# Token-major feed-forwards, output projections and gates in a two-block network on one core

## The chip, the core and the metric

The kernel runs on one core of one Trainium2 chip. The metric is device microseconds of one execution. The engines are TensorE (PE; PEld is its weight-load side), VectorE (DVE), ScalarE (ACT), GpSimd (POOL) and SyncE (SP), whose queue starts all loads here.

## What is computed

256 tokens of 1024 features pass through a block of one layer and a block of two, all in float32. Each `swiglu` is a feed-forward with 2816 inner features; the first block normalises before and after each part, the second only before.

```python
def swiglu(x, w_gate, w_up, w_down):
    return (jax.nn.silu(x @ w_gate) * (x @ w_up)) @ w_down
# first block
f = swiglu(rms_norm(h, ffn1_pre_norm[l]), ffn1_w_gate[l], ffn1_w_up[l], ffn1_w_down[l])
h = h + FFN_RESIDUAL_WEIGHT * rms_norm(f, ffn1_post_norm[l])
mixed = hybrid_mixer(rms_norm(h, mix_pre_norm[l]), ...)       # 8-head attention, 4-head delta rule
h = h + rms_norm(mixed @ w_out[l], mix_post_norm[l])
c = memory_cross_attention(rms_norm(h, mem_pre_norm[l]), rms_norm(mem, mem_kv_norm[l]), ...)  # ends with @ w_o
h = h + rms_norm(c, mem_post_norm[l])
f = swiglu(rms_norm(h, ffn2_pre_norm[l]), ...)
h = h + FFN_RESIDUAL_WEIGHT * rms_norm(f, ffn2_post_norm[l])
# second block, each of two layers
h = h + 0.5 * swiglu_2(rmsnorm(h, ffn1_norm[i]), ffn1_wg[i], ffn1_wu[i], ffn1_wd[i])
h = h + hybrid_mixer_2(rmsnorm(h, mix_norm[i]), ...)
h = h + 0.5 * swiglu_2(rmsnorm(h, ffn2_norm[i]), ffn2_wg[i], ffn2_wu[i], ffn2_wd[i])
gate = jax.nn.sigmoid(rmsnorm(h, ple_norm[i]) @ ple_w_gate[i])
h = h + gate * (p[i] @ ple_w_proj[i])
return rmsnorm(h, final_norm)
# inside hybrid_mixer_2: short convolution and a chunked state-space scan (ssd), then
merged = jax.nn.sigmoid(gate_a) * y_a + jax.nn.sigmoid(gate_m) * y_m   # y_a = .. @ sc_w_out, y_m = .. @ m_w_out
return merged @ w_o
```

## The kernel before

**Layout.** Activations lie feature-major: the residual `h` is eight tiles [128 features, 256 tokens]. A product of the large kind takes each operand in two float32r parts, `hi` and `lo` (`split` for activations, `wunit` for weights), and adds three passes: hi·hi, hi·lo, lo·hi (`mm3`, L325). The weights are stationary, 128 by 128, and 256 tokens stream past them; the sum lands in a PSUM tile [128, 256] of the pool `pm` (four banks). A few products (`proj_tok`, L369: the values of the two attentions) already have tokens on partitions.

**Weights.** `wunit` (L283) loads 512 KB, [128, 4 row chunks, 256 columns], copies it to `hi` on ACT (L297) and subtracts on DVE (L298). There are four raw buffers and three of `hi` and `lo`. The Tile framework orders all instructions by priority, which is program order; units are taken `AHEAD` = 60 places early. `preload` (L306) takes the first units of the next stage further ahead, into tiles of the arena `R`.

**Stages.** `ffn` (L470) goes over 11 column blocks, two 256-column blocks of gate and up at a time; for each 128 features DVE multiplies by the spread reciprocal root `rb`, ACT takes silu, DVE multiplies, ACT and DVE split. The down product then runs over 22 row chunks. `residual` (L508) adds a product to `h`. `post` (L514) is the first block's norm after a part: `evict` squares each chunk, `finish` scales it, adds it to `h` and splits `h` for the next stage.

**Root mean squares.** Features lie on partitions, so squares are summed with one-column products on PE (`rstd` L399, `sum_squares` L439); POOL raises to the power -1/2, and `spread` (L416) multiplies with the identity to bring the 256 token values to every partition.

**Fillers.** Work that waits for nothing stands in the program where a norm is pending: `mem_k` after the first feed-forward and after `w_out`, `ple_proj(0)` after `mem_w_o`, `ple_proj(1)` after the first block's last feed-forward.

**Arenas.** Fixed tiles are handed out in program order: `S` [128, 256], `D` pairs of them, `R` pairs in float32r. `scope` adds tiles for a part.

Of the kernel before, what the change touches and what calls it, by code (L numbers as in the profile page):

```python
# [23 lines left out]
# columns of the packed per-feature vectors (one column per 128 features)  # L24
# [10 lines left out]
# rows that every partition holds  # L35
# [54 lines left out]
# how many places of the program order a weight unit is taken ahead, how many one that preload() takes,  # L90
# and how many places products that wait for other engines are put back
AHEAD = 60
PRELOAD = 120
# [3 lines left out]
class Arena:  # L97
    """fixed tiles, handed out and taken back in program order"""
# [22 lines left out]
    def get(self, keep=False):  # L121
        """keep: a tile that outlives the parts added last"""
# [14 lines left out]
class Net:  # L137
    def __init__(self, ctx, tc, a):
# [12 lines left out]
        self.S.add(ap, 36)  # L151
# [9 lines left out]
        self.ones = {n: self.cst.tile([P, 1], F32, name=f"ones{n}") for n in (1, 128, 512, 1024)}  # L161
        nc.gpsimd.memset(self.ones[1], 1.0)
        for n in (128, 512, 1024):
            self.act(self.ones[n], self.ones[1], AF.Copy, scale=1.0 / n)
        self.h = self.start()
        self.ident = self.c("ident")
        nc.sync.dma_start(self.ident, a["con"][:, :P])
# [5 lines left out]
    def constants(self):  # L173
# [7 lines left out]
        # masks and selectors, exact in bfloat16  # L181
# [11 lines left out]
    def start(self):  # L193
        """the activations in the order that the first products need them, with the first weights between"""
        nc, a = self.nc, self.a
        h = [self.S.get() for _ in range(KC)]
        first = [(a[f"ffn1_w_{q}"], ks) for ks in self.steps(KC) for q in ("gate", "up")]
        self.ahead, units = [], []
        for i in range(3):
            src, ks = first[i]  # L200
# [3 lines left out]
            units.append(self.wunit(src[0, :, ks[0]:ks[-1] + 1, :], len(ks), False, 2 if i == 0 else 1))  # L204
            for c in range(max(4 * i, 1), min(4 * i + 4, KC)):
                nc.sync.dma_start(h[c], a["xT"][c * P:(c + 1) * P, :])
        self.ahead = units[::-1]
        return h

# [15 lines left out]
    def t(self, tag, shape, dtype=F32, bufs=2, part=False):  # L225
        """scratch: the next of bufs fixed tiles; part: only there within the current scope"""
# [8 lines left out]
    def half(self):  # L235
        """scratch [P, 256]: halves of the two t tiles in turn"""
# [11 lines left out]
    def late(self, *names):  # L248
        """products that wait for other engines, put behind others that are ready"""
# [33 lines left out]
    def wunit(self, src, a, prio=True, cut=1):  # L283
        """hi/lo parts of src [P, a, 256], in cut pieces"""
# [3 lines left out]
        n = a * S  # L288
# [3 lines left out]
        with self.tc.high_priority(AHEAD) if prio else nullcontext():  # L292
            for c in range(cut):
                j, e = c * a // cut, (c + 1) * a // cut
                r, o, d = (q[:, j * S:e * S] for q in (raw, hi, lo))
# [3 lines left out]
        parts = [x[:, :n].rearrange("p (a b) -> p a b", a=a) for x in (hi, lo)]  # L299
        return [[q[:, j] for q in parts] for j in range(a)], []  # L300

    def first(self, *src):
        """the units that come first when the first blocks of src are taken in step"""
        return [(q, 0, ks) for ks in self.steps(KC) for q in src]

    def preload(self, *units):  # L306
        """the parts of units (src, block, row chunks), which are the next to be used, in tiles of the arena"""
        nc, out = self.nc, []
        for src, b, ks in units:
            n = len(ks)  # L310
            with self.tc.high_priority(PRELOAD):
                raw = self.wp.tile([P, 1024], F32, tag="raw", name="raw", bufs=4)
                nc.sync.dma_start(raw[:, :n * S].rearrange("p (a b) -> p a b", a=n), src[b, :, ks[0]:ks[-1] + 1, :])
                tiles = [self.split(raw[:, j * S:(j + 1) * S], keep=True) for j in range(n)]
            out.insert(0, ([[t[:, 0, :], t[:, 1, :]] for t in tiles], tiles))
        return out

    def units(self, src, b, K):
        """the weight units of column block b of src [blocks, P, K, 256]: row chunks, hi/lo parts"""
        for ks in self.steps(K):  # L320
            w, tiles = self.wunit(src[b, :, ks[0]:ks[-1] + 1, :], len(ks))
            yield ks, w
            self.R.put(*tiles)
# [8 lines left out]
    @staticmethod  # L332
    def steps(K):
        """the row chunks of each weight unit"""
        return [range(k, min(k + 4, K)) for k in range(0, K, 4)]
# [10 lines left out]
    def proj(self, src, b0, nblk, x, evict, wide=False, last=False):  # L346
        """evict(chunk, ps) with ps [P, 256]: out features on partitions; wide: the first two blocks in step;
        last: the chunks of the last block one after the other"""
        u = 0
        while u < nblk:  # L350
            if last and u == nblk - 1:
                units = list(self.units(src, b0 + u, len(x)))
                for f in range(2):
                    ps = self.mbank()[:, :S]
                    for ks, w in units:
                        for k, wk in zip(ks, w):
                            self.mm3(ps, wk, x[k], k == 0, k == len(x) - 1, f * P)
                    evict(2 * u + f, ps)
                return
# [8 lines left out]

    def proj_tok(self, src, b0, nblk, x, evict):  # L369
        """evict(blk, t, ps) with ps [P, 256]: tokens of tile t on partitions"""  # L370
        K = len(x)
        for u in range(nblk):
            banks = [self.mbank()[:, :S] for _ in range(2)]
            for ks, w in self.units(src, b0 + u, K):
                for t in range(2):
                    for k, (wh, wl) in zip(ks, w):
                        xh, xl = x[k][:, 0, t * P:(t + 1) * P], x[k][:, 1, t * P:(t + 1) * P]
                        self.mm(banks[t], xh, wh, k == 0, False)
                        self.mm(banks[t], xl, wh, False, False)
                        self.mm(banks[t], xh, wl, False, k == K - 1)  # L380
# [9 lines left out]
    def sq_acc(self, acc, src):  # L390
        """acc + src*src for src [P, 256] (acc None to begin)"""
# [1083 lines left out]
```

## Time and profile before

| | us |
|---|---|
| median of 3 runs | 2219.32 |
| lowest and highest run | 2210.61, 2225.4 |
| span of the profiled execution, first to last instruction | 2217.7 |
| PE busy in it | 2195.2 |

The page gives the profiled execution by its span only; that is 1.6 us under the median run. Busy PE time counts modelled ends, so a stretch in which PE is busy throughout can still issue its products at different rates: rates are read as time over count.

### The profile page before, as it was taken

To read this page: it belongs to the slowest core of one execution; us is meant where nothing else is said; L and a number is where in the kernel's file an instruction comes from. 1 tells how busy PE (TensorE), PEld (TensorE's weight loads), DVE (VectorE), ACT (ScalarE), POOL (GpSimd) and SP (SyncE) were. 2 spreads that over 40 slices of the span, in tenths; PEclk is the share of its full clock that TensorE was granted. 3 is DMA by queue.
4 is the path that set the end of the run, shared out by engine and by line. 5 is a ranking of instruction groups with operands and counts; after the bars stand their busy time and mean duration, and the time that the engine had idled before them with its cause. 6 is when DMAs were issued, how large, how long until landed. Compare 5 with 4: busy or idle time off the path is not lost.

```text
span 2217.7 us, 45480 instructions
## 1 busy us (share of the span) xinstructions
PE 2195.2 (99%) x18672; PEld 2152.2 (97%) x18672; DVE 1558.5 (70%) x2608; ACT 1185.1 (53%) x2033; POOL 43.3 (2%) x54
## 2 busy tenths in 40 slices
PE   8999999999999999999999999999999999999998
PEld 8999997999999999998999999999999999999998
DVE  6756873667665766798766766676669886767666
ACT  6545633555454544567555554454457755645444
POOL 0000000000000000000000000000000000000000
PEclk9999997999999999999999999999999999999999
DMA  7565520435556556553455556655665436555563
GB/s 255 177 185 169 166 77 1 166 121 162 189 184 191 173 188 186 186 186 106 157 189 185 192 190 195 190 182 195 190 196 187 136 125 193 179 193 193 193 188 127
DMA packets 110369, 379.44 MB, mean 171 GB/s; under 512 B 12368, under 2 KB 17104, under 8 KB 110160
## 3 DMA queue, kind: packets, MB, share of 16 engines
q1 hardware_dynamic: 110160, 376.53, 52.9%
q8 instruction: 146, 2.39, 0.4%
q14 instruction: 63, 0.52, 0.1%
HBM read 375.43 MB, written 1.05 MB: 170 GB/s over the span
## 4 chain that ended last, share of the span: by engine, by line
PE 95%; DVE 2%; ACT 1%; DMA 1%; issue 0%; POOL 0%; SPq 0%; DVEq 0%; ACTq 0%; POOLq 0%
PE pm L265 84%; PE px L265 11%; PE px L268 1%; DVE lo L298 1%; DVE s L259 0%; DMA raw<-in_ffn_w_up_dram 0%; DMA raw<-in_ple_w_gate_dram 0%; ACT hi L297 0%; DMA raw<-in_ffn_wu_dram 0%; DVE r L259 0%; ACT d L262 0%; PE pm L268 0%; ACT L262 0%; DVE acc L256 0%; DVE w L253 0%
## 5 line engine op out<-in xcount | busy, mean ns | idle before, releaser
L265 PE MATMUL pm<-r,hi 128*128 128x256 f32 x10640 | 1861.5, 279 | 7.2 <-ACT hi L297 5.7
L265 PEld LDWEIGHTS pm<-r,hi 128*128 128x128 f32 x10640 | 1621.7, 189 | 9.5 <-ACT hi L297 5.7
L265 PE MATMUL pm<-r,lo 128*128 128x256 f32 x5320 | 1484.4, 279 | 1.6 <-DVE lo L298 1.6
L298 DVE TENSOR_TENSOR lo<-raw,hi 128x1024 fp32r<-128x1024 f32 (+1 forms) x718 | 861.0, 1200 | 488.3 <-ACT hi L297 484.4
L297 ACT CAST hi<-raw 128x1024 fp32r<-128x1024 f32 (+1 forms) x718 | 739.1, 1030 | 731.5 <-PE pm L265 576.5
L265 PEld LDWEIGHTS pm<-r,lo 128*128 128x128 f32 x5320 | 1001.4, 188 | 3.2 <-DVE lo L298 2.2
L276 ACT CAST r<-w 128x256 fp32r<-128x256 f32 x136 | 54.5, 403 | 61.0 <-DVE w L253 61.0
L253 DVE TENSOR_TENSOR t<-pm,rb 128x512 f32<-128x512 f32 (+1 forms) x132 | 80.4, 636 | 0.2
L262 ACT ACTIVATE r<-s,vec 128x256 fp32r<-128x256 f32 x136 | 66.1, 504 | 22.1 <-DVE s L259 18.2
L262 ACT ACTIVATE sq<-s 128x256 f32<-128x256 f32 x152 | 60.3, 410 | 27.6 <-DVE s L253 19.8
L259 DVE SCALAR_TENSOR_TENSOR s<-pm,vec,s 128x255 f32<-128x255 f32 x144 | 68.9, 479 | 2.8
L259 DVE SCALAR_TENSOR_TENSOR r<-s,vec,r 128x256 fp32r<-128x256 f32 x136 | 65.5, 499 | 5.0 <-ACT r L262 4.4
L265 PE MATMUL px<-r,hi 128*128 128x256 f32 x384 | 66.9, 279 | 0.0
L277 DVE TENSOR_TENSOR r<-w,r 128x256 fp32r<-128x256 f32 x136 | 57.0, 422 | 8.1
L265 PEld LDWEIGHTS px<-r,hi 128*128 128x128 f32 x384 | 58.5, 189 | 0.0
L265 PE MATMUL px<-r,lo 128*128 128x256 f32 x192 | 53.5, 278 | 0.0
L413 POOL TENSOR_TENSOR rs<-rv,mhalf 128x2 f32<-128x2 f32 x26 | 23.4, 898 | 1504.2 <-DVE rv L411 1504.2
L262 ACT ACTIVATE w<-t 128x256 f32<-128x256 f32 x132 | 48.1, 409 | 7.1 <-DVE t L253 7.1
L253 DVE TENSOR_TENSOR w<-w,t 128x256 f32<-128x256 f32 x132 | 50.1, 418 | 0.3 <-ACT w L262 0.2
L265 PE MATMUL px<-d,d 128*64 128x128 f32 (+2 forms) x384 | 42.7, 291 | 0.2
L256 DVE TENSOR_TENSOR acc<-acc,sq 128x256 f32<-128x256 f32 x94 | 39.4, 420 | 4.4 <-ACT sq L262 1.9
L262 ACT ACTIVATE d<-px,nac 128x128 f32<-128x128 f32 x128 | 36.4, 375 | 3.2 <-PE px L265 2.9
(231 smaller groups left out, 1371.8 us busy)
## 6 DMA issues: line engine op xcount, KB each, us to landing
raw<-in_w_in_dram SPq DMA_DIRECT2D x188, 512.0 KB, 3.8
raw<-in_ffn_wg_dram SPq DMA_DIRECT2D x88, 512.0 KB, 4.5
raw<-in_ffn_wu_dram SPq DMA_DIRECT2D x88, 512.0 KB, 4.5
raw<-in_ffn_wd_dram SPq DMA_DIRECT2D x80, 512.0 KB, 4.0
raw<-in_ffn_w_up_dram SPq DMA_DIRECT2D x44, 512.0 KB, 4.5
raw<-in_ffn_w_gate_dram SPq DMA_DIRECT2D x43, 512.0 KB, 4.6
raw<-in_ffn_w_down_dram SPq DMA_DIRECT2D x40, 512.0 KB, 3.6
raw<-in_m_w_out_dram SPq DMA_DIRECT2D x32, 512.0 KB, 4.4
```

The lines of the kernel that those rows point to most:

```text
L253: self.nc.vector.tensor_tensor(out=out, in0=a, in1=b, op=ALU.mult)
L256: self.nc.vector.tensor_tensor(out=out, in0=a, in1=b, op=ALU.add)
L259: self.nc.vector.scalar_tensor_tensor(out=out, in0=a, scalar=s, in1=b, op0=op0, op1=op1)
L262: self.nc.scalar.activation(out, a, f, **kw)
L265: self.nc.tensor.matmul(out, lhsT=lhsT, rhs=rhs, start=start, stop=stop)
L268: self.nc.tensor.transpose(out, a, self.ident[:k, :k])
L276: nc.scalar.copy(hi, src)
L277: nc.vector.tensor_tensor(out=lo, in0=src, in1=hi, op=ALU.subtract)
L297: nc.scalar.copy(o, r)
L298: nc.vector.tensor_tensor(out=d, in0=r, in1=o, op=ALU.subtract)
L413: self.nc.gpsimd.tensor_tensor(out=r, in0=v, in1=self.mhalf[:, :2], op=ALU.pow)
```

## The change

Feed-forwards, `w_out`, `mem_w_o`, the two attentions' values, the second mixer's two gates, `sc_w_out`, `m_w_out`, `w_o` and the embedding gate and projection become token-major: `tblock` takes 128 tokens of an activation chunk as the stationary operand and streams 512 weight columns into a whole PSUM bank, once for each half of the tokens. Gate and up columns are laid side by side in memory (`beside`). The residual `h` becomes two tiles [128 tokens, 1024]. Sums of squares become a by-product of an ACT square (`sq_row`), and the reciprocal root is a per-partition scalar (`rstd_row`) that ACT or DVE applies at eviction, without `spread`. Where the next product needs features on partitions, PE transposes (`turn`, `close`). Gains of the norms after a part come as a row broadcast to all partitions (`row`). `preload` goes; `ple_proj(1)` moves from the end of the first block to ahead of the second layer. The projections into the mixers (`proj`), the memory's queries and keys, and the scans stay feature-major. Lines of the diff that only drop comments are left out.

```diff
-        self.S.add(ap, 36)
+        self.S.add(ap, 12)
+        self.T = Arena("tk", [P, D], F32)
+        self.T.add(ap, 6)
...
+            units.append(self.wunit(a["ffn1_gu"][0, :, ks[0]:ks[-1] + 1, :], False, 2 if i == 0 else 1))
+            for c in range(max(2 * i, 1), 2 * i + 2):
                 nc.sync.dma_start(h[c], a["xT"][c * P:(c + 1) * P, :])
+            for c in range(2 * i, 2 * i + 2):
+                x.append(self.split(h[c], self.v("ffn1_pre_norm", c)))
...
+        for t in range(2):
+            nc.sync.dma_start(self.h[t], a["x"][t * P:(t + 1) * P, :])
...
-    def preload(self, *units):
-        """the parts of units (src, block, row chunks), which are the next to be used, in tiles of the arena"""
-        nc, out = self.nc, []
...
+        step = 1024 // src.shape[3]
...
+    def tblock(self, src, b, x, banks):
+        K = len(x)
+        for ks, w in self.units(src, b, K):
+            for t in range(2):
+                s = slice(t * P, (t + 1) * P)
+                for k, (wh, wl) in zip(ks, w):
+                    xh, xl = x[k][:, 0, s], x[k][:, 1, s]
+                    self.mm(banks[t], xh, wh, k == 0, False)
+                    self.mm(banks[t], xl, wh, False, False)
+                    self.mm(banks[t], xh, wl, False, k == K - 1)
+            yield ks
...
+    def turn(self, src, c):
+        ps = self.bank()
+        for j in range(2):
+            for t in range(2):
+                self.transpose(ps[:, j * S + t * P:j * S + (t + 1) * P], src[t][:, (c + j) * P:(c + j + 1) * P])
+        return ps.rearrange("p (j s) -> p j s", j=2)
...
-    def rstd(self, acc, n, mult=1.0):
...
+    def sq_row(self, ss, t, n, src, mult=1.0):
+        junk = self.t("junk", [P, W], bufs=1)
+        self.act(junk, src, AF.Square, scale=(mult / D) ** 0.5, accum_out=ss[:, n, t:t + 1])
+    def rstd_row(self, ss, mult=1.0):
...
+        self.stt(v, ss[:, 0], EPS * mult, ss[:, 1], ALU.add, ALU.add)
         r = self.t("rs", [P, 2])
         self.nc.gpsimd.tensor_tensor(out=r, in0=v, in1=self.mhalf[:, :2], op=ALU.pow)
         return r
...
+    def turned(self, src, gain=None):
+        x = []
+        for c in range(0, KC, 2):
+            ps = self.turn(src, c)
+            x += [self.split(ps[:, j], None if gain is None else self.v(gain, c + j), True) for j in range(2)]
+        return x
...
+    def row(self, name):
+        g = self.t("grow", [P, D], bufs=1)
+        self.nc.sync.dma_start(g, self.a["rows"][self.a["row_of"][name]:self.a["row_of"][name] + 1, :].to_broadcast([P, D]))
...
+    def lend(self, n):
+        tiles = [self.T.get() for _ in range(n)]
+        new = [t[:, j * W:(j + 1) * W].rearrange("p (a s) -> p a s", a=2) for t in tiles for j in range(2)]
+        self.D.free[:0] = new
+        self.D.parts.append(new)
...
-    def ffn(self, x, acc, wg, wu, wd, evict, mid=None):
-        with self.scope(NF, 0, 0):
-            rb = self.rstd_b(acc, D)
-            rbb = rb[:, None, :].to_broadcast([P, 2, S])
...
+    def ffn(self, x, ss, wgu, wd, evict, mid=None):
+        with self.scope(0, 0, 0) as pool:
+            with self.late("rstd"):
+                r = self.rstd_row(ss)
...
+            def close(gt):
+                ps = self.bank()
+                for f in range(2):
+                    for t in range(2):
+                        self.transpose(ps[:, f * S + t * P:f * S + (t + 1) * P], gt[:, t, f * P:(f + 1) * P])
+                n = len(g)
+                d = pool.tile([P, 2, 2, S], F32R, tag=f"g{n}", name=f"g{n}", bufs=1)
+                psv = ps.rearrange("p (f s) -> p f s", f=2)
+                self.nc.scalar.copy(d[:, 0], psv)
+                self.nc.vector.tensor_tensor(out=d[:, 1], in0=psv, in1=d[:, 0], op=ALU.subtract)
+                g.extend([d[:, :, 0], d[:, :, 1]])
+            last = None
...
-                for f in range(2):
...
-                    g.append(self.split(sg))
+                banks = [self.mbank() for _ in range(2)]
+                for ks in self.tblock(wgu, u, x, banks):
+                    if ks[0] == 2 and last is not None:
+                        close(last)
+                gt = self.t("t", [P, 2, S])
+                for t in range(2):
+                    self.act(gt[:, t], banks[t][:, :S], AF.Silu, scale=r[:, t:t + 1])
+                    self.stt(gt[:, t], banks[t][:, S:], r[:, t:t + 1], gt[:, t], ALU.mult, ALU.mult)
+                last = gt
                 if mid and u in mid:
                     mid[u]()
...
+            banks = [self.mbank() for _ in range(2)]
+            g += [None, None]
+            gg = Late(g, lambda: (g.__delitem__(slice(-2, None)), close(last)))
+            for d in range(D // W):
+                if d:
+                    banks = [self.mbank() for _ in range(2)]
+                for _ in self.tblock(wd, d, gg, banks):
+                    gg.settle()
+                for t in range(2):
+                    evict(d, t, banks[t])
...
-        """evict that adds scale*ps to h in place"""
-        def evict(c, ps):
-            self.stt(h[c], ps, scale, h[c], ALU.mult, ALU.add)
+        def evict(n, t, ps):
+            o = h[t][:, n * W:(n + 1) * W]
+            self.stt(o, ps, scale, o, ALU.mult, ALU.add)
...
-            f = self.S.get()
-            self.nc.vector.tensor_scalar(out=f, in0=ps, scalar1=self.v(gain, c), scalar2=None, op0=ALU.mult)
-            st["f"].append(f)
...
+        st = dict(f=[self.T.get() for _ in range(2)], ss=self.t("ss", [P, 2, 2]), g=self.row(gain))
+        def evict(n, t, ps):
+            s = slice(n * W, (n + 1) * W)
+            self.sq_row(st["ss"], t, n, ps, mult)
+            self.mul(st["f"][t][:, s], ps, st["g"][:, s])
...
+            r = self.rstd_row(st["ss"], mult)
+            ss = self.t("ss", [P, 2, 2])
...
+            for n in range(2):
+                s = slice(n * W, (n + 1) * W)
+                for t in range(2):
+                    self.stt(h[t][:, s], st["f"][t][:, s], r[:, t:t + 1], h[t][:, s], ALU.mult, ALU.add)
+                for c in range(4 * n, 4 * n + 4, 2):
+                    ps = self.turn(h, c)
+                    x += [self.split(ps[:, j], self.v(gain, c + j), True) for j in range(2)]
+                for t in range(2):
+                    self.sq_row(ss, t, n, h[t][:, s])
...
+        for t in range(2):
+            nc.vector.tensor_scalar(out=hn[t], in0=h[t], scalar1=r[:, t:t + 1], scalar2=None, op0=ALU.mult)
...
+        def ga_evict(n, t, ps):
+            self.act(ya[t][:, n * W:(n + 1) * W], ps, AF.Tanh, scale=rh[:, t:t + 1])
+        self.proj_tok(a["w_in_2_gates"][i], 0, 1, xu, ga_evict)
+        x = self.turned(hn, "mix_norm_2" + L)
+        self.T.put(*hn)
+        self.proj_tok(a["w_in_2_gates"][i], 1, 1, xu, lambda n, t, ps: ga_evict(1, t, ps))
...
+        def ym_evict(n, t, ps):
+            o = gm[t][:, n * W:(n + 1) * W]
+            self.stt(o, o, 1.0, ps, ALU.add, ALU.mult)
+            self.add(o, o, ya[t][:, n * W:(n + 1) * W])
+            if t:
+                for c in range(4 * n, 4 * n + 4, 2):
+                    p2 = self.turn(gm, c)
+                    merged.extend(self.split(p2[:, j]) for j in range(2))
+        self.proj_tok(a["m_w_out_2"][i], 0, 2, yn, ym_evict)
+        self.T.put(*gm, *ya)
         self.R.put(*yn)
-        self.proj(a["w_o_2"][i], 0, 4, merged, self.residual(h, 0.5))
...
-            mixed = self.mixer1(h, *x)
+            with self.lend(6):
+                mixed = self.mixer1(h, *x)
             ev, fin = self.post("mix_post_norm", 1.0)
...
-        w = self.preload(*self.first(a["ffn1_wg_2"][0], a["ffn1_wu_2"][0])[:2])
-        self.ple_proj(1)
-        self.ahead = w
+        self.ffn(*x, a["ffn2_gu"], a["ffn2_w_down"], ev)
         return fin(h, "ffn1_norm_2.0")
...
+        if i:
+            n.ple_proj(1)
+            x = n.pre(h, f"ffn1_norm_2.{i}")
...
+    for b in range(2):
+        for t in range(2):
+            n.sq_row(ss, t, b, h[t][:, b * W:(b + 1) * W])
+    r = n.rstd_row(ss)
+    for b in range(2):
+        for t in range(2):
+            o = h[t][:, b * W:(b + 1) * W]
+            n.stt(o, o, r[:, t:t + 1], g[:, b * W:(b + 1) * W], ALU.mult, ALU.mult)
+            nc.sync.dma_start(out[t * P:(t + 1) * P, b * W:(b + 1) * W], o)
...
+    def beside(g, u):
+        *lead, k, m = g.shape
+        both = [q.reshape(*lead, k, m // S, 1, S) for q in (g, u)]
+        return np.concatenate(both, axis=-2).reshape(*lead, k, 2 * m)
```

## Rows read from the trace of the kernel before

**Rows 1.** The page, part 1: busy time of each engine.

```profile
PE 2195.2 (99%) x18672; PEld 2152.2 (97%) x18672; DVE 1558.5 (70%) x2608; ACT 1185.1 (53%) x2033; POOL 43.3 (2%) x54
```

**Rows 2.** The page, part 4: shares of the chain that ended last, by engine.

```profile
PE 95%; DVE 2%; ACT 1%; DMA 1%; issue 0%; POOL 0%; SPq 0%; DVEq 0%; ACTq 0%; POOLq 0%
```

**Rows 3.** Windows: stretch, length, each engine's busy us and instructions, PEclk, DMA, GB/s.

```profile
60.00:202.00 142.00, 142.00 (x1205) 141.88 (x1205) 89.67 (x124) 67.53 (x98) 0.26 (x1) 1.00 0.59 183
...
415.00:437.00 22.00, 22.00 (x194) 21.83 (x193) 16.62 (x30) 12.93 (x22) 0.00 (x0) 1.00 0.58 191
...
729.00:925.00 196.00, 196.00 (x1668) 196.00 (x1667) 130.15 (x183) 96.92 (x145) 3.26 (x2) 1.00 0.58 182
...
1190.00:1278.00 88.00, 88.00 (x779) 88.00 (x778) 60.13 (x91) 44.20 (x65) 1.39 (x2) 1.00 0.58 192
...
1484.00:1660.00 176.00, 176.00 (x1555) 176.00 (x1554) 117.27 (x159) 89.80 (x130) 2.59 (x1) 1.00 0.61 193
...
2014.00:2188.00 174.00, 174.00 (x1537) 173.99 (x1536) 115.09 (x156) 86.97 (x126) 0.00 (x0) 1.00 0.61 193
```

**Rows 4.** Groups of PE instructions, shapes apart: busy us, mean ns, idle before.

```profile
L265 PE MATMUL pm<-r,hi 128*128 128x256 f32 x10640 | 1861.5, 279 | 7.2 <-ACT hi L297 5.7 <-DVE r L259 0.9 <-ACT r L262 0.6
...
L265 PE MATMUL px<-ones,acc 128*128 128x1 f32 x152 | 20.5, 228 | 0.8 <-DVE acc L256 0.8
...
L265 PE MATMUL px<-con,rs 128*128 128x128 f32 x100 | 18.1, 284 | 2.5 <-POOL rs L413 2.5
...
L268 PE MATMUL px<-con,s 128*128 128x128 f32 x80 | 11.6, 274 | 0.0
...
L265 PE MATMUL px<-ones,sq 128*128 128x1 f32 x72 | 10.9, 256 | 1.4 <-ACT sq L262 1.4
...
L265 PE MATMUL px<-d,d 128*128 128x256 f32 x32 | 7.4, 379 | 0.0
```

**Rows 5.** Timeline of PE, three stretches: start, us, instruction, count.

```profile
246.04 1.39 PE L265 MATMUL px<-ones,sq 128*128 128x1 f32 x12
...
486.75 3.19 PE L265 MATMUL px<-d,d 128*128 128x256 f32 x14
...
1009.56 0.71 PE L268 MATMUL px<-con,s 128*128 128x128 f32 x5
```

**Rows 6.** What PE waited for: us in total, times, longest.

```profile
PE pm L265 <- ACT hi L297: 5.7, 1, 5.7
```

**Rows 7.** Groups of ACT, DVE and POOL instructions, shapes apart.

```profile
L298 DVE TENSOR_TENSOR lo<-raw,hi 128x1024 fp32r<-128x1024 f32 x684 | 837.7, 1225 | 458.4 <-ACT hi L297 454.5
L297 ACT CAST hi<-raw 128x1024 fp32r<-128x1024 f32 x684 | 718.1, 1050 | 685.6 <-PE pm L265 536.2 <-issue 104.8 <-PE px L265 20.4
L253 DVE TENSOR_TENSOR t<-pm,rb 128x512 f32<-128x512 f32 x108 | 71.5, 685 | 0.0
...
L262 ACT ACTIVATE r<-s,vec 128x256 fp32r<-128x256 f32 x136 | 66.1, 504 | 22.1 <-DVE s L259 18.2 <-DVE s L256 2.0 <-DVE s L253 1.5
...
L413 POOL TENSOR_TENSOR rs<-rv,mhalf 128x2 f32<-128x2 f32 x26 | 23.4, 898 | 1504.2 <-DVE rv L411 1504.2
...
L262 ACT ACTIVATE d<-px 128x512 f32<-128x512 f32 x4 | 2.4, 598 | 1.4 <-PE px L268 1.3
```

**Rows 8.** Windows again: the start, and the stretch at the lower clock.

```profile
0.00:20.00 20.00, 12.12 (x78) 11.39 (x79) 12.14 (x22) 12.79 (x27) 1.72 (x9) 1.00 0.81 269
...
356.00:394.00 38.00, 38.00 (x144) 28.79 (x144) 10.76 (x38) 8.78 (x28) 1.65 (x1) 0.51 0.01 1
```

**Rows 9.** Timeline of PE at two stage changes of block 2.

```profile
1452.15 0.38 PE L265 MATMUL pm<-r,hi 128*128 128x256 f32 x1 [0.86 <-DVE r L259]
...
1479.52 0.61 PE L265 MATMUL px<-ones,acc 128*128 128x1 f32 x4 [0.59 <-DVE acc L256]
```

**Rows 10.** The chain that ended last, its end: start, us, what.

```profile
2199.94 5.57 PE pm L265 x49
...
2212.86 0.78 DVE s L259 x2
```

More of the change, by code (lines that the diff above doesn't have):

```diff
@@ L161, in __init__ @@
         self.ones = {n: self.cst.tile([P, 1], F32, name=f"ones{n}") for n in (1, 128, 512, 1024)}
+        self.h = [self.cst.tile([P, D], F32, name=f"h{t}")[:] for t in range(2)]
         nc.gpsimd.memset(self.ones[1], 1.0)
@@ L196, in start @@
         h = [self.S.get() for _ in range(KC)]
[L197 to L200, printed above, removed]
+        self.ahead, units, x = [], [], []
+        for i, ks in enumerate(self.pairs(KC)):
             if i == 0:
@@ L298, in wunit @@
                 nc.vector.tensor_tensor(out=d, in0=r, in1=o, op=ALU.subtract)
[L299 to L304, printed above, removed]
-    def preload(self, *units):
-        nc, out = self.nc, []
[L309 to L316, printed above, removed]
+        parts = [x[:, :a * n].rearrange("p (a b) -> p a b", a=a) for x in (hi, lo)]
+        return [[q[:, j] for q in parts] for j in range(a)]
     def units(self, src, b, K):
[L320 to L323, printed above, removed]
+        step = 1024 // src.shape[3]
+        for k in range(0, K, step):
+            ks = range(k, min(k + step, K))
+            yield ks, self.wunit(src[b, :, ks[0]:ks[-1] + 1, :])
     def mm3(self, ps, w, x, first, last, m0=0):
@@ L332, in steps, with pairs @@
     @staticmethod
-    def steps(K):
-        return [range(k, min(k + 4, K)) for k in range(0, K, 4)]
+    def pairs(K):
+        return [range(k, min(k + 2, K)) for k in range(0, K, 2)]
     def block(self, src, b, x, banks):
@@ L344, in block, with proj @@
             yield
[L346 removed]
+    def proj(self, src, b0, nblk, x, evict, wide=False):
         u = 0
         while u < nblk:
[L351 to L359 removed]
             n = 2 if wide and u == 0 else 1
@@ L422, in spread, with rstd_b @@
         return ps[:, :S]
-    def rstd_b(self, acc, n, mult=1.0):
-        with self.late("rstd"):
-            r = self.rstd(acc, n, mult)
+    def rstd_b(self, r):
         with self.late("rstd", "spread"):
@@ L540, in finish @@
-            self.S.put(*st["f"])
-            return x, ps
+            for n in range(2):
+                s = slice(n * W, (n + 1) * W)
[6 more added lines that the diff above has]
+                    self.sq_row(ss, t, n, h[t][:, s])
@@ L962, in mem_pre @@
             m.append(t)
-        acc = self.squares(m)
+        acc = None
+        for c in range(KC):
+            acc = self.sq_acc(acc, m[c])
         with self.late("mem"):
-            ps = self.spread(self.rstd(acc, D))
+            ps = self.spread(self.rstd([acc], D))
             x = []
@@ L1333, in block1 @@
             x = fin(h, "mem_pre_norm")
-            o = self.mem_attn(*x)
+            with self.lend(4):
+                o = self.mem_attn(*x)
             ev, fin = self.post("mem_post_norm", 1.0)
-            self.proj(a["mem_w_o"], 0, 4, o, ev)
+            self.proj_tok(a["mem_w_o"], 0, 2, o, ev)
             self.R.put(*o)
-            w = self.preload(*self.first(a["ffn2_w_gate"], a["ffn2_w_up"])[:2])
             self.ple_proj(0)
-            self.ahead = w
             x = fin(h, "ffn2_pre_norm")
-        if upto < 4:
-            return
@@ L1358, in block2, with __init__, __len__, __getitem__ @@
             self.mixer2(h, i, pool)
-        if upto < 7:
-            return
-        self.ffn(*self.pre(h, "ffn2_norm_2" + L), a["ffn2_wg_2"][i], a["ffn2_wu_2"][i], a["ffn2_wd_2"][i], self.residual(h, 0.5))
+        self.ffn(*self.pre(h, "ffn2_norm_2" + L), a["ffn2_gu_2"][i], a["ffn2_wd_2"][i], self.residual(h, 0.5))
         with self.scope(0, 0, 0):
-            self.ple(h, i, i == 1)
-def body(ctx, tc, a, out, upto=99, start=1):
+            self.ple(h, i)
+class Late:
+    def __init__(self, made, make):
+        self.made, self.make = made, make
+    def __len__(self):
+        return len(self.made)
+    def __getitem__(self, k):
+        return self.made[k]
+    def settle(self):
+        if self.make:
+            self.make()
+            self.make = None
@@ L1367, in body @@
+def body(ctx, tc, a, out):
     n = Net(ctx, tc, a)
@@ L1469 @@
         a[name] = nc.dram_tensor(f"in_{name}_dram", v.shape, mybir.dt.from_np(v.dtype), kind="ExternalInput").ap()
-    out = nc.dram_tensor("out_0_dram", (D, S), F32, kind="ExternalOutput").ap()
+    a["row_of"] = {n: i for i, n in enumerate(_ROWS)}
+    out = nc.dram_tensor("out_0_dram", (S, D), F32, kind="ExternalOutput").ap()
     with tile.TileContext(nc) as tc, ExitStack() as ctx:
```

353 lines of the change are left out of this document (130 added, 223 removed).

## The prediction

> **What bounds the kernel now.** I read the engines' shares first, then the chain, then windows of dense stretches. PE is busy 99% and its weight-load side 97%, DVE 70%, ACT 53% [rows 1]; 95% of the chain that ended last is PE [rows 2]. So PE sets the time, and the question is at which rate it issues. In stretches where it never pauses, time over count gives 142.0/1205 = 117.8 ns and 196/1668 = 117.5 ns a pass in the feed-forwards of the first block and the first of the second; 176/1555 and 174/1537 = 113.2 ns in later ones; 113.4 ns in `w_out` and 113.0 ns around `sc_w_out` and the z columns [rows 3]. All stream 256 columns, which at the granted full level, 2.4 GHz, is 106.7 ns. What is the rest? One-column products, which stream nothing, still start (1.39 - 0.256)/11 = 103 ns apart [rows 4, 5]: each brings a 128 by 128 load of its own, so loads alone pace PE at nearly the rate of the present passes. A longer stream behind each load should hide it. The nearest row with such a stream is the attention's 128x256 float32 instruction. It lasts 379 ns against 279 ns for the float32r pass of the same shape, about another 256 columns longer, so it streams 512 columns' worth. Fourteen of them start (3.19 - 0.379)/13 = 216 ns apart [rows 4, 5], which is 512 columns at 2.4 GHz and 3 ns. PE otherwise waits for little: its largest wait is 5.7 us for the first weights [rows 6].
>
> **The change: passes.** One feed-forward has 44 column chunks x 8 row chunks x 3 passes for gate and up and 8 x 22 x 3 for down, 1584; six have 9504. The projections that change have 3456: `w_out` and `mem_w_o` 192 each, values 288, and per layer gates 384, `sc_w_out` 192, `m_w_out` 384, `w_o` 192, embeddings 240. Before: three feed-forwards at 117.6 (558.8 us), three at 113.2 (537.9), 3456 at about 114 (394.0): 1490.7 us. After, half as many passes of twice the columns: 6480 x 216.2 = 1401.0. That is -89.7 us. No row shows a float32r pass of 512 columns. The bounds are 213.3 (the stream alone; -108) and 226.4 (two passes at 113.2; -24); I take 216.2, the row with the same stream and the same kind of load. The Trainium skill, page "TensorE: Matmul & The Clock Gate", section "Back-to-back issue gap", gives 131 ns as the sustained rate at 512 columns; by it the passes would take 849 us and the kernel about 1621. The float32 row disagrees, 216 against 131, and I don't use it.
>
> **Products removed.** Of the 152 + 72 one-column instructions 84 stay (memory norm, head norms, the scan's norm), 140 go; of the 100 spreads 40 stay, 60 go [rows 4]. 200 x 103 ns = -20.6 us.
>
> **Transposes added.** Four per column block of a feed-forward: 4 x 11 x 6 = 264. Sixteen each time the residual becomes an operand: 7 calls of `pre`, 4 of `finish`, and 2 each for `hn` and `merged`, 240. In sum 504. Five in a row in the scan start (0.71 - 0.274)/4 = 109 ns apart [rows 5]: +54.9 us, in full on PE. The upper bound is one at a time, 274 ns [rows 4], +138 us; four stand together, so I take 109. The skill's same page, section "PE-mode transpose", gives about 275 ns in a kernel's context; by that price the sum would come out 84 us higher, near 2257. The row agrees with it for the duration of one, 274, and not for the distance between two.
>
> **Other engines.** A weight unit is still 512 KB and now feeds 12 passes, 2.59 us of PE. Its split costs ACT 1.05 and DVE 1.23 us [rows 7]. A feed-forward block of 10.4 us then asks DVE for 4 x 1.23 plus two eviction steps of about 0.5 and one 0.69, some 6.6 us, and ACT for some 5.8: hidden behind PE. Without that cover each unit would be late by its split. The evictions per 512 columns, 0.69 us on DVE [rows 7], replace two of 256; they lie beside PE. `preload` is costed at nothing: the four raw buffers and three pairs of parts stay, and PE waited for a `hi` part once, at the start [rows 6]. If that cover goes, a stage change pays one split, 2.3 us.
>
> **Waits added.** `close` puts its transposes on PE's queue behind the second unit of the next block, 5.2 us after the block they belong to; the four eviction steps they wait for take about 2 us, so nothing should stand. Behind them queue the third unit's passes. On SP's queue the two `x` tiles (1 MB) and the broadcast gain rows (0.5 MB each) are new. At the start loads move 269 GB/s at 0.81 of the DMA engines, and PE is busy for only 12.1 of 20 us [rows 8]: 1.5 MB there is 0 to 5.6 us; I take +2, since the first unit needs fewer bytes. At the end of `ffn2` of the first block `ple_proj(1)` no longer covers the norm: square 0.60, POOL 0.90, two DVE steps of 0.69, four transposes 0.44, ACT split 0.50 [rows 7] make 3.8 us without handovers. I take +5; the bounds are 3.8 and 8, the upper one if the granted clock falls in that gap to 1.2 GHz, as it does in [rows 8] after thinly filled products. Six other changes (`residual`, then `pre`) wait for one 512-column eviction, two transposes and a split, 0.69 + 0.22 + 1.0 us, behind which 8 to 16 transposes are useful work: 0.7 each, +4, bounds 0 and 12. Before, such changes cost 0.86 and 0.59 us [rows 9]: -1.5. The tail from the last product to the end is 2217.7 - 2205.5 = 12.2 us now [rows 10]; after, tanh, two DVE steps, a square, POOL and up to four DVE steps are as long within 2 us: 0.
>
> **Sum.** -89.7 - 20.6 + 54.9 + 2 + 5 + 4 - 1.5 = -46 us. The profiled span of 2217.7 becomes 2172; the median run lies 1.6 above that span, so 2173.
>
> **Rivals.**
> (a) The stage changes eat the gain. With token-major data a norm ends with the last bank, and transposes sit between it and the next product. If all eleven changes paid the full 5 us instead of one, 55 - 9 = +46: 2219. Against it: three of the four `finish` calls still have a filler, and block two's norms are applied at eviction. For it: the removed `preload`.
> (b) Slower: the feed-forward's transposes reach PE's in-order queue before their evictions are done, because the framework moves them. Then each of 66 `close` calls stops PE for ACT 0.5, DVE 0.5 and a second such pair partly, about 1.5 us: +99, 2272. It decides from 46/66 = 0.7 us a call. Against it: the program places them 5.2 us late.
> (c) The change does not do what it says: the overhead grows with columns, and a pass takes 2 x 113.2. Then only the slow feed-forwards and some projections gain, -24 instead of -89.7: 2239. The 216 ns row speaks against it, with a different data type.
> (d) More: the 38 us at 0.51 of the clock [rows 8], where the first block's heads run, are reordered so that the clock holds: up to -19, 2154. Nothing in the change aims at it, and the same could go the other way. The 4032 passes that stay at 256 columns may also fall to 117.6 or 113.2: -4 to +14.
>
> **How the numbers follow.** Forecast 2173, chance 0.66 (its own range 2155 to 2196); (a) 0.13; (b) 0.05; (c) 0.05; (d) 0.10; the rest lies outside. The range of 8 in 10 goes from 2147, which takes in (d) and the lower bounds, to 2209, which takes in half of (a) and the upper bounds of the stalls; (b), (c) and the rest stay out. About 1% (22 us) is what a measurement of this kernel tells from no change, its runs being 15 us apart. Faster than 2197: the forecast, (d) and a small part of (a), 0.78. Slower than 2241: (b) and half of (c)'s spread, 0.06. Between: 0.16.
>
> **What would show it.** Right: PE near 12,500 products; dense feed-forward windows at 216 ns a pass, PEld share near a half; transposes about 109 ns apart; one gap of about 5 us before the second block. Wrong: passes above 220 ns, PE waiting for `t` in the middle of feed-forwards, PE waiting for splits at stage changes, or a lower granted clock in new places.

## The result and the profile after

The changed kernel takes 2288.24 us (median of 4 runs, 2285.4 to 2290.07) against 2214.97 (4 runs, 2209.08 to 2225.4): 1.032 times as long, interval 1.0286 to 1.0353. It is slower; the forecast was 2173. The profiled execution took 2285.4 us, its span is 2283.6.

The page of the changed kernel, parts 1 and 4 (shares of the chain by engine):

```profile
PE 2254.1 (99%) x12496; PEld 1908.3 (84%) x12496; DVE 1403.2 (61%) x2073; ACT 1183.8 (52%) x1892; POOL 37.2 (2%) x54
...
PE 95%; DVE 2%; ACT 1%; DMA 1%; issue 0%; SPq 0%; POOL 0%; POOLq 0%; DVEq 0%; ACTq 0%
```

PE issues a third fewer instructions than in [rows 1], 12,496, and is as busy and as much of the chain as in [rows 2]. So each takes longer than forecast, or PE stands more. The waits say which (engine and line; who for; us in all, times, longest):

```profile
PE pm L276 <- ACT hi L308: 6.8, 2, 5.3
PE px L279 <- DVE h L270: 5.0, 2, 4.5
PE pm L276 <- DVE r L270: 5.0, 10, 1.2
PE pm L276 <- ACT r L273: 0.6, 1, 0.6
```

Those are the weights at the start as in [rows 6], the uncovered finish and the stage changes, some 11 us beside the start. It is not standing. The chain that ended last, two of its rows in the last feed-forward's region (start, us, what):

```profile
2076.72 11.20 PE pm L276 x48
...
2123.28 11.20 PE pm L276 x48
```

48 passes of 512 columns in 11.20 us are 233.3 ns each, where I had put 216.2. Windows of the changed kernel (stretch, length, busy us and count by engine, PEclk, DMA share, GB/s) show that the clock isn't the reason:

```profile
722.00:730.00 8.00, 5.61 (x22) 4.86 (x23) 6.09 (x14) 5.27 (x15) 1.39 (x2) 0.57 0.37 135
1200.00:1300.00 100.00, 99.68 (x449) 80.02 (x449) 59.82 (x76) 48.37 (x70) 1.39 (x2) 1.00 0.57 179
1484.00:1660.00 176.00, 175.90 (x785) 141.92 (x784) 97.90 (x111) 87.78 (x118) 0.69 (x1) 1.00 0.55 181
```

The dense stretches are granted 1.00, the 2.4 GHz level, as in [rows 3]. The first row is the finish before the second block.

The whole account follows from PE's start times. Each product gets the time to the next one's start. Of a float32r pass, what goes beyond 1.35 times its usual price (113.3 or 233.3) counts as waiting.

```
us (count)                       before             after
float32r passes, 256 columns     1956.1 (16,992)     472.7 (4032)
float32r passes, 512 columns                        1512.7 (6480)
waiting and gaps                   36.8               46.1
one-column products, spreads       33.6 (325)         12.3 (126)
transposes of t, h, tk              0.8 (6)           56.1 (540)
other products                    177.4 (1348)       168.5 (1318)
before the first, from the last    13.0               15.5
```

30 of the transposes of `tk` were there before under another name, among the others.

### The profile page after: what moved, and what is told of

It reads as the page before. It is cut to its first block, busy times and chain, and to the rows that moved or that the text cites. A ratio compares the mean times of both kernels' runs of the same rounds, so it can differ in the third digit from the quotient of the medians.

```text
span 2283.6 us, 32381 instructions
## 1 busy us (share of the span) xinstructions
PE 2254.1 (99%) x12496; PEld 1908.3 (84%) x12496; DVE 1403.2 (61%) x2073; ACT 1183.8 (52%) x1892; POOL 37.2 (2%) x54
## 4 chain that ended last, share of the span: by engine, by line
PE 95%; DVE 2%; ACT 1%; DMA 1%; issue 0%; SPq 0%; POOL 0%; POOLq 0%; DVEq 0%; ACTq 0%
PE pm L276 86%; PE px L276 7%; PE px L279 2%; DVE lo L309 1%; DMA raw<-in_ffn_gu_dram 1%; ACT hi L308 1%; DVE h L270 0%; DVE s L270 0%; DVE r L270 0%; PE pm L279 0%; ACT L273 0%; ACT d L273 0%; POOL rk L696 0%; ACT s L273 0%; DVE d L264 0%
## 5 line engine op out<-in xcount | busy, mean ns | idle before, releaser
L276 PE MATMUL pm<-hi,r 128*128 128x512 f32 x3264 | 1041.5, 399 | 11.9 <-ACT hi L308 6.8
L276 PEld LDWEIGHTS pm<-hi,r 128*128 128x128 f32 x3264 | 608.9, 189 | 158.7 <-DVE r L270 9.0
L276 PE MATMUL pm<-lo,r 128*128 128x512 f32 x1632 | 647.2, 397 | 0.5 <-DVE lo L309 0.5
L276 PE MATMUL pm<-r,hi 128*128 128x256 f32 x2688 | 487.8, 282 | 0.5 <-DVE r L270 0.5
L276 PEld LDWEIGHTS pm<-r,hi 128*128 128x128 f32 x2688 | 414.1, 189 | 3.0 <-DVE r L270 1.0
L276 PE MATMUL pm<-r,lo 128*128 128x256 f32 x1344 | 378.4, 282 | 0.0
L276 PEld LDWEIGHTS pm<-lo,r 128*128 128x128 f32 x1632 | 307.4, 188 | 74.4 <-DVE lo L309 1.2
L276 PE MATMUL pm<-hi,g 128*128 128x512 f32 x1056 | 332.4, 396 | 0.0
L276 PEld LDWEIGHTS pm<-r,lo 128*128 128x128 f32 x1344 | 253.3, 188 | 1.0 <-issue 0.7
L276 PE MATMUL pm<-lo,g 128*128 128x512 f32 x528 | 208.7, 395 | 0.0
```

The source lines that it names most:

```text
L276: self.nc.tensor.matmul(out, lhsT=lhsT, rhs=rhs, start=start, stop=stop)
```

## Experiments

Three theories for the 233.3 ns stood at first: the price is the columns' own (A), the load's (B), or that of traffic at SBUF (C).

**m_quiet, m_traffic: passes alone.** The body of the kernel is replaced by blocks of one shape; the second has a stream of weight units beside them.

```
+ sec("a512", 144, tok, tokw(512), 512)        # xh wh, xl wh, xh wl, as in tblock
+ sec("c384", 144, tok, tokw(384), 384)        # and 256, 128 columns; half stationary;
+ sec("h512bf", 144, ...)                      # one stationary; bfloat16; float32
+ for u in range(220): n.wunit(...)            # m_traffic alone
```

> The network is left out; only blocks of equal passes run, each block 144 or 288 passes of one shape, no other engine at work and no DMA under way, with the output a copy of the input. Theory A (a float32r column itself costs about 0.456 ns, so the price is proportional to the columns): 512 columns 233 ns, 384 columns 175, 256 columns 117, 128 columns about 109 or the load of the stationary. Theory B (each pass pays a fixed toll for loading its stationary, about 20 ns over 213.3): 512 columns 233, 384 columns 180, 256 columns 127, and a stationary of 64 columns, or the same stationary each time, is cheaper than 233 by up to 17 ns. Theory C (traffic of the other engines and of the DMAs at SBUF slows the stream): here, with none, 512 columns take 216 and 256 columns take 109 to 113. bfloat16 at 512 columns: A and B leave it open, 213 to 216 if only float32r pays. Behind these, 34 short blocks of 96 passes at 256 columns, each after another event (a float32 product of 1, 128, 256 or 512 columns, two of them, a bfloat16 product, an idle gap): each block is expected to keep one of the two prices 113.3 and 117.8, and the event that goes ahead of a change is what sets it.

> The network is left out; the same blocks of 144 or 288 passes as in the quiet run (without the short blocks at the end), beside a stream of 220 weight units that belongs to nobody (DMA of 512 KB, ScalarE's copy, VectorE's subtraction, as in the kernel). Theory C (traffic): 512 columns 233 ns here and 216 in the quiet run, and the 256-column blocks rise from 113 to 118. Theories A and B: every block takes within 1 ns what it takes in the quiet run.

PE's timeline of m_traffic (start, us, instruction, count; us less the last pass's own latency, by count less one, is about the distance of starts):

```profile
37.80 33.84 PE L276 MATMUL a<-w,r 128*128 128x512 f32 x144
...
71.62 33.84 PE L276 MATMUL b512same<-w,r 128*128 128x512 f32 x144
...
105.43 25.20 PE L276 MATMUL c<-w,r 128*128 128x384 f32 x144
...
130.61 32.91 PE L276 MATMUL d256tok<-w,r 128*128 128x256 f32 x288
...
196.36 32.35 PE L276 MATMUL f<-w,r 128*128 128x128 f32 x288
...
228.75 33.70 PE L276 MATMUL g512half<-w,r 128*64 128x512 f32 x144
...
262.42 31.24 PE L276 MATMUL h512bf<-xb 128*128 128x512 bf16 x144
...
293.64 31.60 PE L276 MATMUL i256bf<-xb 128*128 128x256 bf16 x288
...
325.22 31.15 PE L276 MATMUL j512f<-xf 128*128 128x512 f32 x72
```

From start to start, once a block runs: float32r 233.3 ns at 512 columns, 173.3 at 384, 113.3 at 256, 111.7 at 128; bfloat16 215.8 and 109.2; float32 at 512, 429.2. Theory B falls: a fixed toll would make 127 at 256 and 180 at 384 columns, and a stationary of half the columns (g), whose load lasts 135 ns in place of 188, still costs 232.7. The same stationary each time (b, loaded anew for each pass) costs 233.3. Windows, m_quiet first, then m_traffic:

```profile
37.00:70.00 33.00, 33.00 (x143) 26.42 (x142) 0.00 (x0) 0.00 (x0) 0.00 (x0) 1.00 0.00 1
```

```profile
38.00:71.00 33.00, 33.00 (x142) 26.59 (x142) 21.03 (x18) 18.94 (x18) 0.00 (x0) 1.00 0.84 281
```

No DMA, or 0.84 of the DMA engines with both other engines busy: 143 and 142 passes in 33 us. Theory C falls too. Theory A is right that the price goes with the columns, but not in proportion: it wanted 117 at 256 and 175 at 384. From 256 columns on, 128 more cost 60.0 ns, where 128 columns at 2.4 GHz are 53.3. bfloat16 pays 2.5 ns a pass beside its columns. The short blocks behind them all lay at 113.3 or 117.8: at 113.3 behind a single float32r product of 512 columns (2 of 2), and once each behind a float32 product of one column (1 of 6) and of 128 (1 of 2).

**a_split: two passes of 256 for one of 512**, from the changed kernel.

```
- self.mm(banks[t], xl, wh, False, False)
+ for c in range(2):
+     o = slice(c * S, (c + 1) * S)
+     self.mm(banks[t][:, o], xl, wh[:, o], False, False)    # likewise the other two
```

> The changed kernel with each pass of 512 streamed columns cut into two passes of 256 columns on the same stationary (but for the first and the last pass of each sum, about 450 of 6480), everything else the same. Were the loss in the pass length itself (the price grows faster than the columns, theory D), two passes at 113.3 to 117.8 would cost 226.6 to 235.6 against 233.3: about -40 us to +14 us, 2248 to 2302. Theory A (proportional to the columns): 2 x 117 = 234, no change within 10 us. Theory B (a fixed toll of 20 ns for each load): 2 x 127 = 253, +120 us, 2410. That the loss is in the passes at all is told by the sign alone: stalls at the stage changes would stay as they are, and the time with them.

2278.84 us (1.0276 of before, 1.0239 to 1.0314), 9.4 less than the changed kernel. By PE's start times the 12,056 halves average 115.8 ns: 231.6 a pair. Theory B's 2410 is out of the question; theories A and D can't be told apart here. The wide pass buys nothing over two narrow ones with the same stationary.

**a_turn2: transposes doubled.**

```
+ for _ in range(2):
      self.transpose(ps[:, ...], src[t][:, ...])    # in turn
```

> The changed kernel with each of the transposes of the residual and of the merged gates made twice into the same place (264 of the 504 that the trace of the changed kernel has a name for; those of the feed-forwards are left single). As I priced them (109 ns each, nothing hidden): +28.8 us, about 2314 to 2319. Rival: the transposes' cost lies in waits around them and not in their passes, then doubling costs less than 10 us. Rival: they also disturb the passes behind them (a refill of the stream), then over +45 us.

The count in that text is wrong: `turn` makes 240 of the 504, so 240 x 109 = 26.2 us was due. 2305.58 us, 17.3 more than the changed kernel. Its PE groups:

```profile
L279 PE MATMUL px<-con,h 128*128 128x128 f32 x352 | 42.0, 279 | 4.5 <-DVE h L270 4.5
...
L279 PE MATMUL px<-con,tk 128*128 128x128 f32 x158 | 21.4, 275 | 0.6 <-DVE tk L1040 0.6
```

By start times 240 more cost 24.7 us on PE, 103 ns each, and waiting gave 4.5 back. The price of 109 holds within 6 ns, neither rival does, and the passes of 512 columns stay at 233 ns.

**m_sizes: where the extra nanoseconds sit.** More blocks of one shape, and pairs of blocks with other products between.

```
+ for c in (512, 448, 320, 256, 192, 160): sec(f"q{c}", 144, tok, tokw(c), c)
+ sec("s512k32", 144, ...[:32], ...[:32], 512)       # 32 partitions; another with 64
+ f32(256)(); sec("base", 60, fea, feax, 256); rr(512, k)(); sec(..., 60, fea, feax, 256)
```

> The network is left out; only blocks of equal float32r passes, no other engine at work, the output a copy of the input. The quiet run gave 111.7, 113.3, 173.3 and 233.3 ns at 128, 256, 384 and 512 columns, with or without traffic, and 109.2 and 215.8 for bfloat16 at 256 and 512. Theory E (a pause of 6.67 ns at each 128 columns after the first, in float32r alone): 448 columns 186.7 + 20 = 206.7 or, if the fourth stretch must be whole, 200; 320 columns 146.7, 192 columns about 112, 160 columns about 112. Theory F (a steady rate of 0.469 ns a column, less 6.7): 448 columns 203.3, 320 columns 143.3, 192 columns about 112. Theory G (the pauses come from the bytes that the 128 partitions read): with operands of 64 and of 32 partitions the 512-column pass falls toward 216; theories E and F leave it at 233. Then 17 pairs of 60 passes at 256 columns: the first of a pair behind a float32 product of 256 columns (117.8 expected), the second behind one to six float32r products of 192 to 512 columns, four float32 transposes or one to three float32 products of one column. Theory H (a float32r pass of 512 columns sets the quick price of 113.3, as it did 2 times of 2): 113.3 behind each of those with 512 columns, 117.8 behind most others. Rival: the price is drawn anew at each interruption, and one in five is quick, whatever stands there.

448 columns took 202.2 ns, 320 took 146.7, 192 and 160 took 111.7, 64 partitions 233.3. Call 6.67 ns beyond the bare columns a pause (the name is for the excess; no row shows one inside a pass). 146.7 at 320 and 173.3 at 384 are then two pauses; 113.3 at 256 is one, 233.3 at 512 three. That is theory E (F wants 143.3 at 320), except at 448, which lies between its two values and 1.1 ns from F's. G, the bytes of all partitions together, has nothing for it at 64 partitions. The bytes that each partition gives in a pass, twice those of bfloat16, remain as a rival: no block tells them from the data type. In the block with 32 the granted clock fell:

```profile
205.00:264.00 59.00, 59.00 (x140) 45.40 (x138) 0.00 (x0) 0.00 (x0) 0.00 (x0) 0.50 0.00 1
```

At 0.50, 1.2 GHz, the pass took 426.7 ns, which is 512 columns and no pause at all, so that block can't be set beside the others. It isn't the 32 partitions: on all 128 the changed kernel's first passes behind its finish, at the lower level until 729.5 us, start 427 ns apart too (its timeline stands with the uncovered finish below). So 512 columns show the pauses at the full clock and none at the lower one. Why, no run shows, but one more block of m_sizes, which the expectation doesn't name, bears on it. 256 columns that are every other one of 512 took 229 ns a pass by PE's start times, at the lower level (to 269 us) and at the full one alike, where 256 neighbouring ones take 113.3 at the full one. How the columns lie in memory can thus set a float32r pass's time, whatever the clock; that the pauses have the same origin is not shown. In the pairs, a single product of 512 columns was followed by 113.3 in 3 of 3, and two, three, four and six in a row by 117.8. A single float32 product of one column was followed by 113.3 in 1 of 2, every other event by 117.8. So theory H holds for singles alone, and something besides them can set the quick price.

**a_bf, b_bf: both kernels in bfloat16.**

```
- F32R = mybir.dt.float32r
+ F32R = mybir.dt.bfloat16
```

> The changed kernel with both parts of every split operand kept in bfloat16 in place of float32r (its results are less exact), everything else the same. If the price of the 512-column pass is what went wrong: 6480 x (233.3 - 215.8) = -113 us, and 4032 x (117.8 - 109.2) = -35 us for the 256-column passes, about 2140 us, and the blocks' passes at 216 and 109 ns as in the quiet run. Rival (stalls or the other engines set the pace, and the passes were only stretched): the time falls by less than 60 us.

> The kernel before with the same replacement of float32r by bfloat16. 12,960 x (115.0 - 109.2) = -75 us and 4032 x (116 - 109.2) = -27 us, about 2113 us. Against the changed kernel in bfloat16 this gives the change without the float32r price: passes 6480 x 215.8 - 12,960 x 109.2 = -17 us, transposes +55, statistics -20, so still +18 to +27 us slower. Rival (the price of the 512-column pass is the whole of the loss): the two are equal or the changed one is quicker.

2140.69 us (2138.65 to 2148.5) for the changed kernel and 2122.37 (2119.62 to 2127.2) for the one before: 0.9629 (0.9602 to 0.9656) and 0.954 (0.9511 to 0.9569) of before in float32r. Both prices come out as in the blocks, 216 and 109 ns. Windows of a_bf, then of b_bf:

```profile
1400.00:1500.00 100.00, 99.25 (x472) 47.52 (x481) 62.90 (x74) 56.59 (x81) 0.70 (x1) 1.00 0.62 195
```

```profile
1400.00:1500.00 100.00, 98.23 (x900) 87.89 (x899) 73.75 (x112) 50.66 (x78) 0.70 (x1) 1.00 0.58 186
```

The changed kernel falls by 147.6 us where 148 was expected, so the price of its passes is what it pays. And the change is 18.3 us slower even in bfloat16 (18 to 27 expected): there 512 columns cost what two passes of 256 cost, less 2.5 ns, and the transposes outweigh the rest. So the price of the 512-column pass is most of the loss and not the whole of it. b_bf beats both kernels, with operands that keep fewer bits.

**b_set, b_set2, b_set3, a_set: what sets 113.3 or 117.8.** Idle products of 512 columns between 256-column passes (in the trace 23 places, not 20): one, two in a row, and one at four chosen places of the kernel before; one in the changed kernel.

```
+ if f == 0 and self.f32_at is not None and self.blocks - self.f32_at >= 3:
+     self.f32_at = None
+     self.mm(self.bank(), w[0][0][:, :P], x[ks[0]].rearrange("p a s -> p (a s)"))
```

> The kernel before with 20 idle float32r products of 512 columns (their sum is not used) put between passes of 256 columns, each a few blocks behind a float32 product, everything else the same. They cost 20 x 0.24 = 5 us. Theory H (one such product puts the 256-column passes into the quick price of 113.3 ns until the next float32 product): most of the 6701 passes that the trace of before has at 117.8 go to 113.3, up to 6701 x 4.44 = -30 us, with the 5 us a net -10 to -25 us, and the slow stretches from 23 to 222 us and from 531 to 925 us are quick for the most part. Rival (the price is drawn at random by each interruption): the slow share stays between 25% and 55%, the time within 8 us of before.

> The control to the run with single ones: at the same 20 places two idle products of 512 columns in a row, 10 us in all. In the small blocks two in a row left the price at 117.8. Theory H: no stretch is made quick by them, the time is before +10 us or more. Rival (any interruption by a float32r product of 512 columns does it, or a random draw): the same slow share as with single ones, the time 5 us above that run's.

> The kernel before with only four of the idle 512-column products, the second, fourth, eighth and eleventh of those in the run with singles, near 60, 260, 537 and 911 us. There a single one turned the price over at 19 of some 21 places, from 117.8 to 113.3 and as often back, and two in a row left it as it was. Theory I (each single one turns the price over, and nothing else differs): the stretches from 63 to about 200, from 260 to 410 and from 537 to 905 us are quick, the fourth gives the rest of the trace its prices of before; some 3500 of the 6701 passes at 117.8 go to 113.3: -15 us, less 1 us for the four, about 2200 to 2208. Rival (the price is drawn by other events and the agreement of the last run was chance): within 6 us of before, with slow shares as before from 531 to 925 us.

> The changed kernel with one idle float32r product of 512 columns near the start of the first mixer's 256-column passes (about 210 us), all else the same. In the trace of the changed kernel 3499 of its 256-column passes lie at 117.8 ns and 382 at 113.3. Theory I (a single one turns the price over until something else turns it): most of the 3499 go to 113.3, up to -15 us, about 2273 to 2280 against 2288. Rival (the products of 512 columns that follow set the price anew): only the first stretch to 350 us changes, 580 passes, -2.6 us, 2285.

2234.0 us for singles (1.0062, 1.0039 to 1.0085), 2225.57 for pairs (1.0021, 0.9999 to 1.0044), 2215.79 for four (0.9987, 0.9964 to 1.001), 2288.23 for the changed kernel with one (1.0322, 1.0288 to 1.0356). Windows of before, of b_set and of b_set2:

```profile
540.00:704.00 164.00, 164.00 (x1395) 164.00 (x1394) 104.44 (x140) 76.74 (x110) 0.69 (x1) 1.00 0.60 188
```

```profile
540.00:704.00 164.00, 164.00 (x1449) 164.00 (x1448) 107.11 (x145) 79.72 (x119) 0.00 (x0) 1.00 0.63 192
...
1185.00:1260.00 75.00, 75.00 (x640) 75.00 (x638) 49.57 (x74) 36.80 (x52) 0.00 (x0) 1.00 0.60 186
```

```profile
540.00:704.00 164.00, 164.00 (x1394) 163.92 (x1393) 104.11 (x139) 76.42 (x110) 0.70 (x1) 1.00 0.60 188
```

One idle product at 537 us makes the next 164 us quick (113.2 ns), a pair leaves them slow (117.6), and the singles in the quick second half made it slow (75.00/640 = 117.2, against 113.0 in [rows 3]). Theory H, that one makes passes quick, falls: it turns them over, and the singles cost 0.6% where H wanted 10 to 25 us off. Each of b_set3's four turned the price, at 60 and 534 us to 113.3, at 257 and 911 us to 117.8. But the trace left the quick price at 709 us with no such product there, and theory I's 2200 to 2208 failed: the traced run took 2203.18, the lowest of 12, and over all 12 the gain is within the interval of none. In a_set the product turned nothing (117.8 before and behind). What sets the price stays open; singles turned it at most places, but not at all of them.

## Why the prediction was wrong

**The failed step** is the price of a pass: "I take 216.2, the row with the same stream and the same kind of load". It is 233.3. 6480 x 17.1 = 111 us: 1512.7 where I had 1401.0. With 1401.0 in its place the span would be 2283.6 - 111.7 = 2171.9, and I had forecast 2172. That it fits so closely is partly luck: transposes and other products came out 8.5 us under their forecast, and the 256-column passes, costed at nothing, 8.5 us over. One term was mis-sized by far the most, and the change's main gain has the other sign: 12,960 passes at the 115.1 of the trace before were 1492 us, so the passes got 21 us dearer instead of 90 cheaper.

**What stood behind it.** I read the distance from 106.7 to 113.3 as the load's, which "a longer stream behind each load should hide". The blocks show otherwise: float32r pays 6.67 ns at most further stretches of 128 columns, so the excess grows with the stream, and half the stationary saves 0.7 ns. The float32 instruction that I priced by has the load and the length of the stream, but not the data type. The upper bound failed for the same reason: "two passes at 113.2" hold one pause each, the wide one three. Rival (c), "the overhead grows with columns", is the mechanism, with chance 0.05 and a price of 226.4 that was still 7 ns short.

The Trainium skill, "TensorE: Matmul & The Clock Gate", section "Back-to-back issue gap", gives N/2.4 + 2.5 ns for an isolated product. That is 109.2 and 215.8, which the bfloat16 blocks take to a tenth of a nanosecond and in a dense stream; the section's 131 ns for a sustained stream of 512 columns shows in no run here, and it says nothing of float32r.

**The other steps**, in their order:
- Removed products, -20.6: the account has 33.6 - 12.3 = 21.3 for 199. Right.
- Transposes, 109 ns each and all on PE, +54.9: the named ones take 56.1/540 = 104 each, the doubled ones 103. Right. They rose by 55.3, of which 30 were there before; with the other products' -8.9 the two lines make +46.4, 9 us under.
- Nothing stands behind `close` (rival (b)): no wait for `t` is among PE's longest. Right; that rival ended near the measured time, by another way.
- The uncovered finish, +5 with bounds 3.8 and 8. PE's timeline of the changed kernel there:

```profile
719.53 0.40 PE L276 MATMUL pm<-lo,g 128*128 128x512 f32 x1
724.39 3.91 PE L279 MATMUL px<-con,h 128*128 128x128 f32 x16 [4.45 <-DVE h L270]
727.95 1.20 PE L276 MATMUL pm<-hi,r 128*128 128x512 f32 x2
728.95 0.63 PE L276 MATMUL pm<-lo,r 128*128 128x512 f32 x1
729.37 0.71 PE L276 MATMUL pm<-hi,r 128*128 128x512 f32 x2
```

  4.45 us of standing, and 16 transposes in 3.91 us at a granted 0.57 where 16 x 109 is 1.7: near 7 us, the upper bound for the reason given with it.
- Start, stage changes and tail, +2, +4 and 0: with the finish forecast 11 less 1.5. Measured: waiting +9.3, ends +2.5. Right, so rival (a) has no place.
- The 4032 passes that stay at 256 columns, costed at nothing, with -4 to +14 named: 472.7 against 464.2 at the former mean, +8.5. In the changed kernel 3499 of them lie at 117.8.
- Rival (d): the stretch at the lower clock was 38 us in [rows 8] and did shrink. Window of the changed kernel:

```profile
367.00:392.00 25.00, 25.00 (x101) 20.34 (x102) 6.89 (x23) 6.18 (x19) 1.65 (x1) 0.52 0.03 9
```

  That is part of the other products' -8.9, and the finish's low clock takes some of it back.
- Of the signs, 12,496 products and the one gap before the second block came as named. "PEld share near a half" didn't: it is 84%, at 188 to 189 ns a float32r load. Near a half it is in bfloat16 alone (47.52 of 100 us in a_bf's window).

## What to carry to other kernels

Price an operation by a row of its own data type, and where none is in the trace let the bounds say so: here the nearest row had the right shape and the wrong type, and 17 ns times 6480 turned a gain of 46 us into a loss of 66. Before replacing narrow passes by wide ones, find out whether the excess over the bare columns belongs to the pass or to the column; a block of 144 equal passes at three widths tells it in 100 us. Transposes between the layouts cost about 0.1 us each on PE and are hidden by nothing when PE is the bound.

## What the runs showed of the hardware

- float32r streams at the full clock with pauses: 113.3, 146.7, 173.3 and 233.3 ns at 256, 320, 384 and 512 columns (all but 320 measured with traffic too). At 1.2 GHz 512 columns take 426.7 ns, with none.
- 256 float32r columns that are every other one of 512 take 229 ns at either clock.
- bfloat16 has none: 109.2 and 215.8 ns.
- 256 float32r columns have two prices, 113.3 and 117.8 ns, that hold for hundreds of passes. In the traced execution of the kernel before 6701 passes lay at the second, worth 30 us, so its own runs may differ by such draws; only the traced ones show it.
- From 192 columns down to 128 a float32r pass with a load of its own gets no cheaper, 111.7 ns.
